# A hybrid decoder layer on one core: the first loads and the first product in another order, and the turned rows of x kept for the residual instead of being turned again

## The chip, the core and the metric

The kernel runs on one core of a Trainium2 chip, as one launch. The metric is device time in microseconds (us). The engines go by the profile's names: PE is TensorE (matrix products and transposes), DVE is VectorE, ACT is ScalarE, POOL is GpSimd, SP is SyncE, which here only issues DMAs. PE's weight loads (PEld) overlap its matmuls.

## What is computed

One inference step of one decoder layer: a prompt of 512 tokens and a sample group of 8 sequences with 4 tokens each, 544 token columns in all, with a model width of 1024.

```
h = RMSNorm_pre(x)
[x_r | q | k | v | g] = h @ W_in
A: x_r -> causal conv (4) -> RG-LRU (8 gate blocks, a scan over the tokens)
B: sliding-window attention, 8 query heads, 2 kv heads, sinks, T5 bias
m = (sigmoid(g_A) * (A @ W_A) + sigmoid(g_B) * (B @ W_B)) @ W_out
x = x + RMSNorm_post(m)                      # x itself is needed a second time here
u = RMSNorm_pre2(x) @ W_up ; causal conv (3)
x = x + RMSNorm_post2((gelu(u_gate) * u_val) @ W_down)
RMSNorm(x, g) = x * rsqrt(mean(x * x) + 1e-6) * g
```

The outputs are the layer's result for prompt and sample and the new recurrent, convolution and key/value states.

## The kernel before, in words

**Layout.** Activations are kept turned: a tile has 128 features on the partitions and the 544 tokens along the row, so the width is KD = 8 tiles. x arrives with tokens on the partitions, in five row blocks (TOK: four of 128 prompt tokens, one of 32 sample tokens), each in two halves of 512 features (x0_0, x0_1, ...). It has to be turned by PE against an identity, through PSUM.

**Products.** Every large product is done in split precision: weights and activations are each a high and a low part (wh, wl; hH, hL), and a weight column of 128 outputs takes three matmuls for each of the 8 k: wh by xh, wh by xl, wl by xh. The tokens are worked in two halves (HALF, 256 and 288 columns; from the lo stage on HALF2, 272 each), so a weight column is 24 matmuls for each half. The high part of a weight is a copy by ACT (`wsplit_hi`, L266), the low part a subtraction by DVE (`wsplit_lo`, L281), in two units of 4 k. `wload` (L246) loads a raw column block of 512 KB on SP's queue into one of five buffers (pool raw); `wclaim` (L256) has two columns loaded ahead.

**Stages.** Norm and turning; the input projection W_in (36 columns, order list L231 to L238, which starts with key, value and query columns 16, 18, 8, 9, 10); in between the attention units, the gates and scans of the RG-LRU, and the products ao (attention output) and lo (recurrent output); then out, the second norm, the up projection, the down projection and the end.

**The start.** `xload` (L357 to L361) issues the x halves on SP, with norm_mix_pre (rows_a) and the first weights among them. 18 dummy matmuls (WARM, tile ps_warm) run on PE meanwhile. `xsquares` (L404) makes sums of squares (ACT tile jk, DVE tile jv), `xrstd` (L412) the factor 1/rms (ss), `xscale` (L417) multiplies each row by it: in tokens-on-partitions form the factor is one number per partition. Then for each k two transposes write ps_ta (L448), and `hsplit` (L431 to L434) makes hH (ACT) and hL (DVE) with the norm's weight pv. The first product, column 16, has an order of its own in `mmhalf` (L315). `norm_b` (L451) does the other 288 tokens later: squares at one tick, factor and scaling at the next, then ps_tb (L461) and hsplit.

**Order.** PE's order is written out by hand throughout (manual_schedule), ACT's and DVE's in the mixer too. `step` (L331) issues one half product and calls `tick` (L194), which splits the next weights and lets side generators go on that were entered with `start_at(t, gen)` (L183); work put on the lists late and last comes after that. SP and POOL take their work in the order in which the program issues it; a waiting instruction holds all behind it on its engine.

**Tables.** `attn_tables` (L544) builds the prompt's bias tables: ps_ohp on PE, rvec on DVE, then on POOL's queue rscr, rrep (both in DRAM) and one btab for each pair of heads (L581). `sample_tables` (L556) makes the sample's bias: 16 copies lt from rel4 on POOL, the tile ohs by DMA, and ps_bs on PE.

**x a second time.** `x_again` (L995 to L1008) reads the row blocks of x again during the lo stage (tile xx, in the raw buffers, L998), turns them on PE (pxx, L1004: 40 transposes in ten groups of four) and copies them to x1[0..7] (L1008, half by ACT, half by DVE). x1 is the residual after the out stage.

PSUM has 3 banks for products (PM) and 5 for the rest (PX); the slots S (52 of 568 columns) hold most activations.

Of the kernel before, what the change touches and what calls it, by code (L numbers as in the profile page):

```python
# [17 lines left out]
P = 128  # L18
# [56 lines left out]
WARM = 18  # L75
# [48 lines left out]
def hawk_step(ctx, tc, I, O):  # L124
# [190 lines left out]
    def mmhalf(ps, key, X, a, ks=range(KD)):  # L315
        n = X.half[a][1] - X.half[a][0]
        if key == order[0] and a == 0:

            for j, (i0, i1) in enumerate(((0, 0), (1, 0), (0, 1))):
                for k in ks:  # L320
                    mm(ps[:, :n], wunits[2 * wpos[key] + k // 4][i0][:, k % 4, :], X.get(k, a, i1),
                       j == 0 and k == 0, j == 2 and k == KD - 1)
            return
        for k in ks:
            wh, wl = (wunits[2 * wpos[key] + k // 4][j][:, k % 4, :] for j in range(2))
            xh, xl = X.get(k, a, 0), X.get(k, a, 1)
            mm(ps[:, :n], wh, xh, k == 0, False)
            mm(ps[:, :n], wh, xl, False, False)
            mm(ps[:, :n], wl, xh, False, k == KD - 1)

    def step(key, X, a, done, target=None, look=2, quick=False):  # L331


        ps = PM("pm" + "_".join(str(z) for z in key) + f"_{a}")
        if quick:
# [27 lines left out]
    xload(0)  # L363
    xload(1)
    nc.sync.dma_start(out=rows_a[0:8, :], in_=I["norm_mix_pre"].rearrange("o (k p) -> (o k) p", p=P))
# [5 lines left out]
    for i in (2, 3, 4):  # L371
        wload(i)
    relx = cp.tile([NBK + 1, NH], F32, name="relx")
    pool.memset(relx, 1.0)
    pool.dma_start(out=relx[0:NBK, :], in_=I["rel_bias"])
    ohp = T("ohp")[:NBK + 1, 0:3 * WIN]
    pool.dma_start(out=ohp, in_=I["c_ohp"])
    for r, nme in ((8, "norm_mix_post"), (16, "norm_ffn_pre"), (24, "norm_ffn_post")):
        pool.dma_start(out=rows_a[r:r + 8, :], in_=I[nme].rearrange("o (k p) -> (o k) p", p=P))
# [6 lines left out]
    pe.transpose(ps0[:, 0:8], rows_a[0:8, :], ident[0:8, 0:8])  # L386
    G_PRE, G_POST, G_FPRE, G_FPOST, C_W, C_B, C_BR, C_BI, C_LAM = 0, 8, 16, 24, 32, 64, 72, 80, 88
# [49 lines left out]
    xsquares(1)  # L437
    xrstd(0, 2)
    split = [wsplit_hi(u) for u in wclaim(2)]
    xscale(0, "av")  # L440
    xscale(1, "vv")
    dve.tensor_copy(pv[:, 0:8], ps0[:, 0:8])
    for u in split:
        wsplit_lo(*u)
    for k in range(KD):
        ps = (PM if k in (5, 6) else PX)(f"ps_ta{k}")
        for i in range(2):
            pe.transpose(ps[:, i * P:(i + 1) * P], xtile(i, k), ident)  # L448
        hsplit(k, 0, ps[:, :256])

    def norm_b():  # L451
        last.extend(lambda i=i: xsquares(i) for i in (2, 3, 4))
        yield
        last.append(lambda: xrstd(2, 5))
        last.extend(lambda i=i, e=e: xscale(i, e) for i, e in ((2, "av"), (3, "av"), (4, "vv")))
        yield
        for k in range(KD):
# [4 lines left out]
            late.append(lambda k=k, ps=ps: hsplit(k, 1, ps[:, :288]))  # L462
# [74 lines left out]
    for t in range(DT):  # L537
        pool.dma_start(out=rel4[32 * t:32 * t + 32, :], in_=I["rel_bias"])
# [379 lines left out]
    start_at(1, norm_b())  # L918
    start_at(2, attn_tables())
# [75 lines left out]
    def x_again(i):  # L995
        t0, n, src = TOK[i]
        x_i = RAW(f"xx{i}")
        nc.sync.dma_start(out=x_i[:n, :], in_=src)  # L998
        yield 2 + i // 4
        for kk in range(2):  # L1000
            px = PX(f"pxx{i}_{kk}")
            for j in range(4):
                k = 4 * kk + j
                pe.transpose(px[:, j * P:j * P + n], x_i[:n, k * P:(k + 1) * P], ident[:n, :n])  # L1004
            yield
            for j in range(4):
                k = 4 * kk + j
                (dve.tensor_copy if j % 2 else act.copy)(x1[k][:, t0:t0 + n], px[:, j * P:j * P + n])  # L1008

    for i in range(5):  # L1010
        start_at(now[0] + 3 + 2 * i, x_again(i))
# [837 lines left out]
```

## Time and profile before

| | |
|---|---|
| median of 3 runs | 1002.92 us (1002.29 to 1003.08) |
| profiled execution | 1003.73 us |
| its span | 1002.0 us |
| busy: PE, DVE, ACT, POOL | 988.9, 732.0, 579.4, 151.0 us |
| first transposes of x (ps_ta) | 11.07 us after the span's start |
| lo stage | 335.66 to 390.40 us |
| mean DMA rate | 133 GB/s |

The span is the profiled execution from its first to its last instruction; the execution's own time holds another 1.7 us around it. In a row of the chain of waits the first number is the start, the second the length, then the engine, tile and line. In a row of the timeline an operation and its shape follow (out <- in, partitions x elements), and in brackets the idle time of the engine before it with what ended it. In a row that groups instructions the three durations are the least, the median and the greatest in ns. In a row of the windows each engine has its busy time with the number of instructions, then the granted PE clock, the mean busy share of the 16 DMA engines and GB/s.

### The profile page before, as it was taken

The numbers are of one execution on the slowest core, as the hardware profiler recorded it, in microseconds if no ns is written. First come the engines' busy times: TensorE is split into PE (matmuls) and PEld (weight loads), VectorE is DVE, ScalarE is ACT, GpSimd is POOL, SyncE is SP. The second block draws the span as 40 slices with busy tenths as digits, with TensorE's granted clock in tenths as the row PEclk, the third lists the DMA queues.
The fourth block names the chain that finished last, engine by engine and source line by source line (L and its number), as shares of the span: only waits on it lengthen the run. The fifth ranks groups of instructions, "written<-read, shape, count | busy, mean of one in ns | idle before, by whom it ended". The sixth has DMA issues, their size and how long they took to land.

```text
span 1002.0 us, 20195 instructions
## 1 busy us (share of the span) xinstructions
PE 988.9 (99%) x7837; PEld 978.5 (98%) x7837; DVE 732.0 (73%) x1555; ACT 579.4 (58%) x1422; POOL 151.0 (15%) x270
## 2 busy tenths in 40 slices
PE   8999999999999999999999999999999999999997
PEld 7999999999999999999999999999999999999996
DVE  6476687545846555589777788888888888887865
ACT  6444455469358535456776756565656565656652
POOL 3131010002304432110001111111111111110004
PEclk9999999999999999999999999999999999999999
DMA  7743223333322345327245858586867676767712
GB/s 211 231 150 93 64 77 105 99 91 94 102 68 85 106 138 148 105 66 210 71 116 124 193 124 192 125 191 127 189 133 184 139 177 145 171 160 167 216 45 90
DMA packets 207687, 133.40 MB, mean 133 GB/s; under 512 B 6546, under 2 KB 194306, under 8 KB 207560
## 3 DMA queue, kind: packets, MB, share of 16 engines
q1 hardware_dynamic: 197944, 112.20, 39.4%
q0 software_dynamic: 9600, 17.90, 11.3%
q10 hardware_dynamic: 48, 2.03, 0.5%
q8 instruction: 61, 1.00, 0.4%
q14 instruction: 34, 0.28, 0.1%
HBM read 111.82 MB, written 9.14 MB: 121 GB/s over the span
## 4 chain that ended last, share of the span: by engine, by line
PE 92%; DVE 3%; ACT 2%; DMA 2%; issue 0%; SPq 0%; ACTq 0%; DVEq 0%
PE pmin L165 22%; PE pmdn L165 16%; PE pux L1400 15%; PE puy L1400 7%; PE pq L1400 6%; PE pmout L165 5%; PE pmao L165 5%; PE pmlo L165 4%; PE puz L1400 4%; PE pg L165 1%; PE psc L165 1%; PE pvp L165 1%; DMA raw_up_s<-in_w_up_dram 1%; DMA raw_in<-in_w_in_dram 1%; PE pt L701 1%; PE ptok L165 1%
## 5 line engine op out<-in xcount | busy, mean ns | idle before, releaser
L165 PE MATMUL pmin<-hH,wh_in 128*128 128x256 f32 (+1 forms) x576 | 167.8, 294 | 0.0
L165 PE MATMUL pmin<-hH,wl_in 128*128 128x256 f32 (+1 forms) x576 | 164.7, 288 | 0.0
L165 PE MATMUL pmin<-hL,wh_in 128*128 128x256 f32 (+1 forms) x576 | 164.6, 288 | 0.0
L165 PE MATMUL pmdn<-fH,wh_dn 128*128 128x256 f32 (+1 forms) x448 | 129.2, 288 | 0.2 <-DVE ft L174 0.2
L165 PE MATMUL pmdn<-fH,wl_dn 128*128 128x256 f32 (+1 forms) x448 | 129.2, 288 | 0.2 <-DVE wl_dn L168 0.2
L165 PE MATMUL pmdn<-fL,wh_dn 128*128 128x256 f32 (+1 forms) x448 | 129.1, 288 | 0.0
L177 DVE SCALAR_TENSOR_TENSOR uc<-u,fv,uc 128x560 f32<-128x560 f32 x128 | 102.0, 797 | 13.3 <-ACT uc L1431 13.2
L165 PEld LDWEIGHTS pmin<-hH,wh_in 128*128 128x128 f32 x576 | 108.9, 190 | 1.9 <-issue 1.2
L165 PEld LDWEIGHTS pmin<-hL,wh_in 128*128 128x128 f32 x576 | 108.1, 188 | 0.0
L165 PEld LDWEIGHTS pmin<-hH,wl_in 128*128 128x128 f32 x576 | 107.9, 188 | 0.0
L165 PEld LDWEIGHTS pmdn<-fH,wh_dn 128*128 128x128 f32 x448 | 84.5, 189 | 0.6 <-issue 0.6
L165 PEld LDWEIGHTS pmdn<-fH,wl_dn 128*128 128x128 f32 x448 | 84.4, 188 | 0.4 <-DVE wl_dn L168 0.4
L165 PEld LDWEIGHTS pmdn<-fL,wh_dn 128*128 128x128 f32 x448 | 84.3, 188 | 0.0
L1526 ACT COPY u<-pux 128x272 f32<-128x272 f32 x52 | 20.1, 387 | 86.1 <-PE pux L1400 86.1
L168 DVE TENSOR_TENSOR u<-puy,u 128x240 f32<-128x240 f32 (+2 forms) x78 | 24.6, 344 | 49.8 <-PE puy L1400 32.1
L174 DVE TENSOR_TENSOR ft<-ft,pmdn 128x256 f32<-128x256 f32 (+1 forms) x104 | 45.2, 436 | 16.7 <-PE pmdn L165 16.1
L277 ACT ACTIVATE wh_in<-raw_in 128x512 fp32r<-128x512 f32 x72 | 44.2, 629 | 19.3 <-PE pmin L165 8.4
L282 DVE TENSOR_TENSOR wl_in<-raw_in,wh_in 128x512 fp32r<-128x512 f32 x72 | 48.2, 683 | 0.8 <-ACT wh_in L277 0.8
L1431 ACT ACTIVATE uc<-u,fv 128x560 f32<-128x560 f32 x64 | 48.2, 754 | 0.0
L664 ACT ACTIVATE s<-s,st 128x256 f32<-128x256 f32 (+1 forms) x32 | 15.2, 475 | 50.4 <-DVE st L661 43.0
L168 DVE TENSOR_TENSOR wl_dn<-raw_dn,wh_dn 128x512 fp32r<-128x512 f32 x56 | 38.3, 684 | 0.0
L1326 POOL DMA_DIRECT2D raw_up_s<-raw_up_s x26 | 22.7, 874 | 102.9 <-issue 5.2
(776 smaller groups left out, 3404.3 us busy)
## 6 DMA issues: line engine op xcount, KB each, us to landing
raw_in<-in_w_in_dram SPq DMA_DIRECT2D x36, 512.0 KB
raw_dn<-in_w_down_dram SPq DMA_DIRECT2D x56, 256.0 KB
raw_up_s<-in_w_up_dram SPq DMA_DIRECT2D x26, 512.0 KB
raw_up_s<-raw_up_s POOLq DMA_DIRECT2D x26, 256.0 KB, 5.9
raw_ao<-in_w_attn_o_dram SPq DMA_DIRECT2D x8, 512.0 KB
raw_lo<-in_w_lru_o_dram SPq DMA_DIRECT2D x8, 512.0 KB
raw_out<-in_w_out_dram SPq DMA_DIRECT2D x8, 512.0 KB
x1d<-x SPq DMA_DIRECT2D x8, 272.0 KB
```

Of the source, the lines that this page charges most:

```text
L165: pe.matmul(out, l, r, start=start, stop=stop)
L168: dve.tensor_tensor(out=out, in0=a, in1=b, op=ALU.subtract)
L174: dve.tensor_tensor(out=out, in0=a, in1=b, op=ALU.add)
L177: dve.scalar_tensor_tensor(out=out, in0=a, scalar=s_, in1=b, op0=op0, op1=op1)
L277: act.activation(hl[0], raw, AF.Copy)
L282: (eng or dve).tensor_tensor(out=hl[1], in0=raw, in1=f32(hl[0]), op=ALU.subtract)
L664: act.activation(s3[:, j, :], s3[:, j, :], AF.Exp, bias=ng[:, j:j + 1], accum_out=sm[:, j:j + 1])
L701: pe.transpose(pt[:, (2 * ch + j) * P:(2 * ch + j + 1) * P], s3[:, j, ch * P:(ch + 1) * P], ident)
L1326: pool.dma_start(out=w["p4"], in_=w["p2"], accum_op=ALU.add)
L1400: pe.matmul(ps[:, :HN], w, x, start=start and k == 0 and i == 0, stop=stop and k == 3 and i == 2, skip_group_check=True)
L1431: act.activation(yt[j][:, 0:FLATU], u[:, 0:FLATU], AF.Copy, scale=fv[:, j:j + 1])
L1526: act.copy(e[nm_], z)
```

## The change

1. *First loads.* SP loads norm_mix_pre ahead of the halves of x1 and no longer behind them. The small loads relx, ohp and three norm weights go from POOL's queue to SP's, ahead of weights 3 and 4; the four loads rel4 go from POOL's to SP's queue.
2. *Dummy matmuls.* WARM goes from 18 to 12; 11 more (KEEP) follow the transpose of norm_mix_pre.
3. *First product.* x0_0, x1_0, x0_1 are scaled by DVE and x1_1 by ACT, ahead of the weight's split; the low parts of column 16 are made by POOL, pv is copied by ACT. The first product's matmuls stand among the transposes ps_ta: the transposes of k, then wh by hH of k-2, then wh by hL of k-3, and all of wl by hH at the end.
4. *ps_ta.* Two k share one PSUM tile (four tiles in all), which stay until they are copied. In the built program the transposes of an odd k wait for the hL of the even k in the same tile, and the hH of an odd k for that hL too.
5. *Kept rows.* The turned, scaled rows are copied from PSUM to xn[0..7]: 8 copies of 128x256 (keep_a) and 8 of 128x288 (keep_b), half by ACT, half by DVE.
6. *Unscaled.* `unscale` takes 1/ss on DVE, sends it to DRAM turned (rmsd, 5 x 128 numbers) and back broadcast over the partitions (rms_full, 128x544), both on SP; POOL multiplies each xn by it and sends it to DRAM (xdram), 272 KB each. On POOL this stands between the first and the second btab.
7. *x a second time.* `x_again` becomes 8 loads from xdram into x1; the loads xx, the 40 transposes and the 40 copies go.

```diff
-WARM = 18
+WARM = 12
+KEEP = 11
...
     xload(0)
+    nc.sync.dma_start(out=rows_a[0:8, :], in_=I["norm_mix_pre"]...)
     xload(1)
-    nc.sync.dma_start(out=rows_a[0:8, :], in_=I["norm_mix_pre"]...)
     wload(0)
     wload(1)
...
     pe.transpose(ps0[:, 0:8], rows_a[0:8, :], ident[0:8, 0:8])
+    for z in range(KEEP):
+        mm(pw[:, (z % 4) * P:(z % 4 + 1) * P], ones, ident, True, True)
...
     xsquares(1)
+    act.copy(pv[:, 0:8], ps0[:, 0:8])
     xrstd(0, 2)
-    split = [wsplit_hi(u) for u in wclaim(2)]
-    xscale(0, "av")
-    xscale(1, "vv")
-    dve.tensor_copy(pv[:, 0:8], ps0[:, 0:8])
-    for u in split:
-        wsplit_lo(*u)
+    u0, u1 = wclaim(2)
...
+    scale0(0, 0)
+    scale0(1, 0)
+    act.activation(xt[1, 1][:, 0:512], xt[1, 1][:, 0:512], AF.Copy, scale=ss[:, 1, 1:2])
+    scale0(0, 1)
+    first_ps = PM("pm_first")
...
+    ps_ta = []
+    wsplit_lo(*wsplit_hi(u0), eng=pool)
+    for k in range(KD + 3):
+        if k < KD:
+            if k % 2 == 0:
+                ps_ta.append(PX(f"ps_ta{k // 2}"))
+            ps = ps_ta[-1][:, k % 2 * 256:k % 2 * 256 + 256]
+            for i in range(2):
+                pe.transpose(ps[:, i * P:(i + 1) * P], xtile(i, k), ident)
+            hsplit(k, 0, ps)
+        if k == 1:
+            wsplit_lo(*wsplit_hi(u1), eng=pool)
+        if 0 <= k - 2 < KD:
+            first_mm(k - 2, 0, 0, start=k == 2)
+        if 0 <= k - 3 < KD:
+            first_mm(k - 3, 0, 1)
     for k in range(KD):
-        ps = (PM if k in (5, 6) else PX)(f"ps_ta{k}")
-        for i in range(2):
-            pe.transpose(ps[:, i * P:(i + 1) * P], xtile(i, k), ident)
-        hsplit(k, 0, ps[:, :256])
+        first_mm(k, 1, 0, stop=k == KD - 1)
...
+    def keep_a(k):
+        (dve.tensor_copy if k % 2 else act.copy)(xn[k][:, 0:256], ps_ta[k // 2][:, k % 2 * 256:k % 2 * 256 + 256])
+
+    def keep_b(k, ps):
+        (act.copy if k % 2 else dve.tensor_copy)(xn[k][:, 256:NT], ps[:, :288])
+
+    def unscale():
+        dve.reciprocal(rms, ss[:, 1, :])
+        nc.sync.dma_start(out=rmsd.rearrange("i p -> p i"), in_=rms)
+        full = S("rms_full")
+        a = rmsd[:, :]
+        nc.sync.dma_start(out=full[:, 0:NT], in_=bass.AP(a.tensor, a.offset, [[0, P], [1, NT]]))
+        yield 2
+        for k in range(KD):
+            pool.tensor_tensor(out=xn[k][:, 0:NT], in0=xn[k][:, 0:NT], in1=full[:, 0:NT], op=ALU.mult)
+            pool.dma_start(out=xdram[k], in_=xn[k][:, 0:NT])
...
     def norm_b():
         last.extend(lambda i=i: xsquares(i) for i in (2, 3, 4))
+        last.extend(lambda k=k: keep_a(k) for k in range(4))
         yield
+        last.extend(lambda k=k: keep_a(k) for k in range(4, KD))
         last.append(lambda: xrstd(2, 5))
...
-            late.append(lambda k=k, ps=ps: hsplit(k, 1, ps[:, :288]))
+            late.append(lambda k=k, ps=ps: (hsplit(k, 1, ps[:, :288]), keep_b(k, ps)))
...
     start_at(1, norm_b())
+    start_at(6, unscale())
...
-    def x_again(i):
-        t0, n, src = TOK[i]
-        x_i = RAW(f"xx{i}")
-        nc.sync.dma_start(out=x_i[:n, :], in_=src)
-        yield 2 + i // 4
...
-    for i in range(5):
-        start_at(now[0] + 3 + 2 * i, x_again(i))
+    def x_again():
+        for k in range(KD):
+            nc.sync.dma_start(out=x1[k][:, 0:NT], in_=xdram[k])
+        yield
+
+    start_at(now[0] + 3, x_again())
```

## What was predicted, with its working

> **What bounds the kernel now.** I read the page's head and its chain first, then the chain cut to the stretches that the change touches, then those stretches engine by engine.
>
> ```profile
> span 1002.0 us, 20195 instructions
> PE 988.9 (99%) x7837; PEld 978.5 (98%) x7837; DVE 732.0 (73%) x1555; ACT 579.4 (58%) x1422; POOL 151.0 (15%) x270
> PE 92%; DVE 3%; ACT 2%; DMA 2%; issue 0%; SPq 0%; ACTq 0%; DVEq 0%
> ```
>
> TensorE is busy in 99% of the span. So a matmul taken off it is worth its own time, and anything that lets it starve costs in full. The change does both: it takes transposes out of the lo stage (a gain that can be read off), and rebuilds the first 35 us, where TensorE starves already.
>
> The chain through the lo stage, 335.66 to 390.40:
>
> ```profile
> 335.66 15.00 PE pmlo L165 x120
> 350.67 0.44 PE pxx L1004 x4
> ...
> 361.00 0.44 PE plr L904 x4
> ...
> 368.50 4.50 DMA xx<-in_x_prompt_dram
> 373.00 0.14 issue
> 373.14 0.63 PE pxx L1004 x4
> ...
> 386.82 0.36 PE pxx L1004 x4
> 387.19 3.21 PE pmlo L165 x24
> 390.40 9.62 PE pmout L165 x77
> ```
> ```profile
> 339.78 0.37 SPq L254 DMA_DIRECT2D raw_lo<-in_w_lru_o_dram  x1
> ```
>
> Ten groups of pxx (the second turning of x) stand in it between blocks of products, and once TensorE waits for a row tile (xx) that comes late. The last row is SP's issue of a late lo weight.
>
> The start, chain first:
>
> ```profile
> 9.26 1.15 ACT wh_in L277 x2
> 11.07 2.90 PE ps_ta L448 x16
> 24.09 2.02 PE ps_tb L461 x12
> 31.18 12.62 PE pmin L165 x96
> 67.39 0.85 PE ps_bs L165 x4
> ```
>
> Up to the first product the path is load, norm, scale, turn; from there it is TensorE in a row, with ps_bs (sample bias, from the tile ohs) in its order.
>
> **The lo stage: gain 5.8.** 390.40 - 335.66 = 54.74 us. The 16 half products are 384 matmuls; at 15.00/120 = 0.125 they need 48.0. Two plr groups stay, 0.88. The rest, 54.74 - 48.0 - 0.88 = 5.86, is ten groups of transposes (eight of 0.44, two of 0.36: 4.24), the wait for xx (about 0.9), and slower refills. In the new program no turning is left; 8 loads of x1 (272 KB each, from DRAM) stand on SP in front of one of the last lo weights. That one went out at 339.78 and its product runs after 373, some 30 us later. They move as many bytes as the x loads that go.
>
> ```profile
> 335.66:390.40 54.74, 53.82 (x435) 53.15 (x434) 29.67 (x70) 24.15 (x61) 18.42 (x19) 1.00 0.43 129
> 372.00:373.00 1.00, 0.22 (x2) 0.00 (x0) 0.00 (x0) 0.00 (x0) 0.51 (x1) 1.00 1.23 371
> ```
>
> The DMA share is 0.43 there, and 371 GB/s was moved in the best us: 2.2 MB take 6 us at that rate, 17 at the stage's mean of 129. Either fits. The 40 copies that go from ScalarE and VectorE were on engines half idle: nothing. I take -5.8; the least is -4.9 (transposes 4.24 and 0.66 of the wait), the most -5.9.
>
> **The start: cost 5.0.** Its rows:
>
> ```profile
> 9.39 1.28 DVE L425 TENSOR_SCALAR x<-x,ss 128x512 f32<-128x512 f32 x3
> 11.55 3.03 ACT L433 ACTIVATE hH<-ps_ta,pv 128x256 fp32r<-128x256 f32 x8 [0.53 <-PE ps_ta L448]
> 12.05 3.23 DVE L177 SCALAR_TENSOR_TENSOR hL<-ps_ta,pv,hH 128x256 fp32r<-128x256 f32 x8
> 14.80 0.47 DVE L177 SCALAR_TENSOR_TENSOR hL<-ps_ta,pv,hH 128x256 fp32r<-128x256 f32 x1
> 18.73 0.42 DVE L168 TENSOR_TENSOR kL<-pmin,kH 128x256 fp32r<-128x256 f32 x1 [0.43 <-ACT kH L599]
> 21.66 1.34 ACT L423 ACTIVATE x<-x,ss 128x512 f32<-128x512 f32 x2 [0.83 <-DVE ss L177]
> 21.66 1.67 DVE L425 TENSOR_SCALAR x<-x,ss 128x512 f32<-128x512 f32 x4
> 27.80 1.28 DVE L282 TENSOR_TENSOR wl_in<-raw_in,wh_in 128x512 fp32r<-128x512 f32 x2
> L501 DVE COPY fv<-ps_rows x1: 415/415/415, 51.9 to 51.9; 128x256 f32<-128x256 f32 x1
> ```
>
> (a) *Earlier turning.* Both x tiles of the first transpose are now first on VectorE and wh follows on ScalarE, so the first turn can start at about 9.39 + 2 x 0.43 = 10.25 instead of 11.07; rows_a ahead of x1 puts up to 0.4 of that back. The 11 added dummy matmuls lie in TensorE's idle stretch before it: nothing, if rows_a lands by about 6.5 (dummies are 0.17 each, 22 instructions, 3.7 us); else up to 0.8.
>
> (b) *Two tiles in one bank.* Before, eight ps_ta had eight PSUM tiles, and hL went every (3.23 - 0.475)/7 = 0.39 us. Now two k share a tile, and the built program ties them: the odd transposes wait for the even hL, the odd hH too. A pair becomes a chain: hL 0.48, turn to hH 0.48 (11.55 - 11.07), hH to hL 0.50 (12.05 - 11.55), next hL 0.39: 1.85 where 0.78 was. With hL0 at 10.25 + 0.98 = 11.23, and the second half of wh_in_16 in between on ScalarE (+0.5), hL7 starts at 11.23 + 4 x 1.85 - 0.39 + 0.5 = 18.7, not 14.80: +3.9. At best, with steps of 0.3 to 0.4 each, a pair is 1.5: +2.5. The first product, spread among the turns, ends 9 matmuls after hL7.
>
> (c) *Copies kept.* keep_a puts four copies 128x256 on each of VectorE and ScalarE ahead of the second norm's scaling. A like copy is 0.41, so 1.3 to 1.7; I take 1.7. From hL7 to the scaling was 21.66 - 14.80 = 6.86; so the scaling comes at 18.7 + 6.86 + 1.7 = 27.3, and its ScalarE part ends 1.34 later, 28.6. ps_tb stood at 24.09: **+4.5**. TensorE gets there at about 27 (19.2, 9 matmuls, another product of 3, ps_ohp, a third of 3), so it is idle for 1.6 us: VectorE and ScalarE bound this stretch, and copies count in full.
>
> (d) *keep_b.* In the split of the second half xn1 and xn3 on ScalarE wait for hL on VectorE, and hH2 queues behind them. From hH0 I follow the two engines step by step (0.35 to 0.5 each): wl_10's first half is done at about 35.8 (27.80 + 0.64 before, with 2.7 us of slack to the product at 31.18). TensorE wants it at 28.6 + 2.02 + 3.06 + 2.02 = 35.7. Slack gone, no wait or 0.5: **+4.5 to +5.0**. The rel4 loads on SP and the lt copies come ahead of the bias tables' chain on GpSimd, which waits for rvec behind the same scaling, and moves like TensorE: nothing beyond.
>
> I take +5.0; from below +3.0 (best pairs, 1.3 for copies), from above +6.5.
>
> Rule against row on KEEP:
>
> ```profile
> 11.00:12.00 1.00, 0.93 (x8) 0.93 (x9) 0.95 (x2) 0.47 (x3) 0.68 (x2) 0.96 1.03 379
> 12.00:13.00 1.00, 1.00 (x7) 1.00 (x6) 0.95 (x3) 1.00 (x5) 0.94 (x8) 0.50 1.08 332
> 15.00:16.00 1.00, 1.00 (x9) 1.00 (x8) 1.00 (x3) 1.00 (x4) 0.00 (x0) 0.83 1.22 290
> ```
>
> The granted clock falls to 0.50 from about 12 to 15.3, after an idle TensorE up to 11.07. The Trainium skill ("TensorE: Matmul & The Clock Gate", Part 1: The HAM clock gate) says that the clock halves after an idle window of about 3.4 us and returns after a busy one; the trace agrees, and by that rule KEEP could hold full clock. Since (b) is bound by hH and hL, full clock would save at most the transposes' half, 4 x 0.18 = 0.7 by the rows; I leave it in the range.
>
> **The unscaling on GpSimd: cost 0.5.** After btab0 GpSimd gets 8 multiplications 128x544 and 8 DMAs; vn, btab1, kout, vout and ohs queue behind.
>
> ```profile
> 42.12 0.76 POOL L581 DMA_DIRECT2D btab<-rrep  x1 [12.73 <-DMA rrep<-rscr]
> 55.31 0.54 POOL L561 DMA_DIRECT2D ohs<-in_c_ohs_dram  x1
> DMA to landing us min/median/max: 2.5/2.5/2.5
> L881 POOL TENSOR_TENSOR xc<-xc,lt x8: 1400/1442/1947, 251.5 to 328.9; 128x568 f32<-128x568 f32 x8
> DMA rscr<-rvec: 3.7, 1
> ```
>
> Start S: btab0 ends at 42.9 + 5 = 48; the factor goes out as rmsd (640 elements of 4 bytes) and comes back as rms_full, issued about 41 and 45 after rows like rscr (3.7 each): 49. So S = 49. Then 8 x (1.45 + 0.75) = 17.6, then vn, btab1, kout, vout and ohs (2.9 together), landing 2.5: ohs is there at 49 + 17.6 + 2.9 + 2.0 = 71.5 to 73.5. TensorE wants it at 67.39 + 5.0 = 72.4: slack of 12 us goes to about none. I take 0.5; the bounds are 0 and 5 (the GpSimd rival).
>
> SP is held between rmsd and rms_full for about 4 us; the weight behind it, (in, 14), comes after four more weight columns of some 6 us each: nothing.
>
> The Trainium skill ("DMA: Bandwidth & Descriptors", Specifications) gives 512 B as the least transfer for line rate, with a read-modify-write below: it speaks against rmsd's 4-byte pieces. No row here shows such a store.
>
> **Sum.** -5.8 + 5.0 + 0.5 = -0.3 on the profiled execution's 1003.73 (span 1002.0 and 1.7 around it): 1003.4. The runs' median, 1002.92, is 0.8 lower; so 1002.6, rounded up for the waits left at nothing: **1002.8**.
>
> **Rivals.**
> - *Front nearly free* (0.22): the tie within a bank is cheaper (pairs of 1.2, hL7 at 16.2) and the copies fit into VectorE's and ScalarE's waits, of which the rows show 0.43 and 0.83. Then the front costs 1 to 2.5: 1002.9 - 5.8 + 2 = 999.1. For: TensorE had 0.8 of slack at ps_tb. Against: the waits in the program.
> - *GpSimd late* (0.18), the slower side: rmsd lands late or the multiplications run at 1.95 like the slowest xc (+4), ohs after 72.4 + x, and TensorE stands x at ps_bs. It decides from S = 50; x of 4 to 5 gives 1002.8 + 4.3 = 1007.1. For: the slack is gone by my sum, and rrep on the same queue took 13 us (12.73 in btab's row). Against: TensorE may itself be later.
> - *Half clock* (0.09): the first product is spread thin over 9 us, and if the clock stays at 0.50 to about 26, the following product costs up to 2.8 more, of which 1.6 is idle anyway; and 1 more if the next goes too: 1005.
> - *The gain isn't had* (0.07): x1's loads hold back the last lo and the first out weights, and the wait for xx comes back as one for a weight: up to 4.5 as xx took: 1006.
>
> Forecast: 0.44. **Range.** From the front nearly free to GpSimd late: 999.0 to 1007.5. It leaves out the cheaper end of the first and the dearer end of the second. **Chances**, with 0.2% (2 us) as what a measurement of this kernel tells from no change: faster 0.26 (0.22 and 0.04 of the forecast's own low end), same 0.40, slower 0.34 (the other three).
>
> **What would show it.** Right: no pxx, and lo 48 to 49 us long; hL in steps of 0.4 and 1.45 by turns, hL7 at 18.7; scaling at 27.3; TensorE idle 1 to 2 us ahead of ps_tb; product (in, 10) done near 39; ohs's issue near 70 with ps_bs soon after. Wrong: hL evenly spaced, ps_tb before 26, a wait of DMA ohs at ps_bs over 1 us, or idle TensorE in lo or out.

## The result and the profile after

| | before | after |
|---|---|---|
| median of 6 runs (lowest to highest) | 1002.79 us (1002.29 to 1003.4) | 1021.78 us (1016.58 to 1023.58) |
| ratio to before | | 1.0176 (95% interval 1.016 to 1.0191) |
| profiled execution, its span | 1003.73, 1002.0 us | 1022.56, 1020.7 us |

The change makes the kernel slower by 19 us, and the prediction (1002.8, at most 1007.5) was wrong. The runs after also spread over 7 us where those before spread over 1. A run more than 1.5% above the fastest of its kernel is slow and is left out of the ratios here and below; there is one, of 1028.75 us, in small_tiny.

The head of the page of after, and the shares of its chain:

```profile
span 1020.7 us, 20162 instructions
PE 995.2 (98%) x7807; PEld 982.4 (96%) x7807; DVE 736.2 (72%) x1541; ACT 578.8 (57%) x1411; POOL 164.7 (16%) x279
PE 87%; DVE 5%; DMA 2%; ACT 2%; issue 2%; SPq 0%; POOL 0%; ACTq 0%; DVEq 0%; POOLq 0%
```

PE had 30 matmuls less and was "busy" 6.3 us longer, at a lower granted clock (0.987 over the span, 0.997 before); its share of the chain fell from 92% to 87%. Rows of the chain of after, cut to the first 90 us and to the lo stage:

```profile
9.60 0.34 PE ps_ta L461
...
13.48 0.69 PE ps_ta L461 x2
14.17 0.43 PE pm_first L166 x2
...
36.17 16.95 issue
53.14 8.10 DMA btab<-rrep
...
70.45 3.53 DVE s L717 x2
...
75.40 5.71 PE pmin L166 x24
...
88.62 0.85 PE ps_bs L166 x4
```
```profile
357.28 23.99 PE pmlo L166 x192
...
406.20 3.88 PE pmout L166 x31
```

Before, PE itself carried the chain from 31 us on. Now it leads through rrep (GpSimd issues it at 35.05 and has it 17 us later), the first btab (8.10 us) and then VectorE, up to 75 us. The same places of both programs, first starts as the trace groups them by tile (us):

| | before | after | later by | added since the row above |
|---|---|---|---|---|
| first transposes (ps_ta) | 11.1 | 9.2 | -1.9 | -1.9 |
| transposes of the second half (ps_tb) | 23.9 | 29.1 | 5.2 | 7.1 |
| first attention scores (psc) | 43.6 | 50.0 | 6.4 | 1.2 |
| sample bias (ps_bs) | 67.2 | 88.5 | 21.3 | 14.9 |
| lo stage (pmlo) | 335.5 | 357.1 | 21.6 | 0.3 |
| out stage (pmout) | 390.2 | 406.0 | 15.8 | -5.8 |
| up projection (pux) | 523.2 | 539.1 | 15.9 | 0.1 |
| the last matmul of the up projection (pux) | 948.1 | 966.9 | 18.8 | 2.9 |
| span | 1002.0 | 1020.7 | 18.7 | -0.1 |

Four terms: the start costs 6.4, the stretch from psc to ps_bs 14.9, the lo stage gives 5.8 back, and 2.9 go at the end of the up projection. These are single profiles: in the runs below with the same first loads and dummies the first turn lies between 9.2 and 10.9, so the row psc of one profile can be off by more than 1 us. What PE waited for in the first 110 us of after (total us, times, longest):

```profile
PE ps_ta L461 <- DVE hL L178: 4.1, 4, 1.6
PE pt L746 <- DVE s L717: 3.7, 2, 2.9
PE pmin L166 <- DVE qL L169: 2.6, 2, 1.7
PE psc L166 <- DVE s L178: 2.5, 1, 2.5
```

The first row is the tie between two k in one PSUM tile. The other three, 8.8 us, are the stretch from 58 to 76: in order of time, 2.5 and 1.7 us follow the late first btab, and 0.9, 2.9 and 0.9 come from 70 to 75, behind VectorE. The rest of its 14.9, some 6 us, goes with half clock, as the windows show: about as many matmuls (191 for 190 before), and no other wait (columns as in the prediction: length, busy time of PE, PEld, DVE, ACT, POOL, then granted clock, DMA share, GB/s):

```profile
58.00:62.00 4.00, 1.46 (x11) 1.22 (x10) 0.62 (x2) 0.00 (x0) 0.00 (x0) 1.00 0.48 80
62.00:66.00 4.00, 2.26 (x13) 2.06 (x14) 2.59 (x7) 2.21 (x10) 2.61 (x2) 0.67 1.01 272
66.00:70.00 4.00, 4.00 (x19) 3.73 (x18) 4.00 (x5) 0.00 (x0) 3.98 (x5) 0.50 0.62 162
70.00:74.00 4.00, 0.33 (x2) 0.14 (x1) 3.93 (x5) 0.00 (x0) 3.98 (x6) 0.93 0.67 254
```

From 66 to 70 PE is busy throughout and gets 19 matmuls done where it got 33 from 50 to 54, at a granted clock of 1.00: that is the half clock. From 64 on VectorE and GpSimd are both busy nearly without a gap.

**What delays the factor and the bias tables.** The queue of SP in after, then windows while rmsd is on its way, and the packets of 53 to 58.2 by queue (number, MB, share of the 16 engines' time; q0 has btab's packets, q1 rmsd's pieces):

```profile
42.97 0.37 SPq L485 DMA_DIRECT2D rmsd<-rms  x1
58.19 0.34 SPq L488 DMA_DIRECT2D rms_full<-rmsd  x1
```
```profile
46.00:49.00 3.00, 3.00 (x25) 3.00 (x24) 1.44 (x3) 1.30 (x3) 0.00 (x0) 1.00 0.46 9
49.00:53.00 4.00, 4.00 (x33) 4.00 (x33) 0.00 (x0) 1.97 (x3) 0.00 (x0) 1.00 0.41 32
```
```profile
q0 software_dynamic: 43, 0.17, 86.0%
q1 hardware_dynamic: 175, 0.00, 2.0%
```

Between the store of rmsd (2.5 KB, 640 pieces of 4 bytes) and the load that waits for it lie 15.2 us. For much of that time the engines are marked busy at 41% and more, and move 9 to 32 GB/s. From 53 to 58.2 they are not busy with the pieces, whose share is 2%: 43 packets of btab hold 86%, that is 5.2 x 16 x 0.86 / 43 = 1.7 us each. Before, from 44.6 to 48.8, 160 packets of that queue (0.52 MB) held 33.8%, 0.14 us each. (Ahead of 53 the pieces share their queue with packets of a weight, whose share can't be told from theirs.) rrep and this btab, on another queue, come late as well: GpSimd waited 12.73 us for rrep before and 16.96 now, and btab takes 8.1 us where the prediction reckoned with 5 for S, the start of the multiplications.

**What the multiplications do to VectorE.** GpSimd, then VectorE, in after:

```profile
67.55 2.64 POOL L491 TENSOR_TENSOR xn<-xn,rms_full 128x544 f32<-128x544 f32 x2
...
71.27 2.62 POOL L491 TENSOR_TENSOR xn<-xn,rms_full 128x544 f32<-128x544 f32 x2
```
```profile
64.40 2.62 DVE L283 TENSOR_TENSOR wl_in<-raw_in,wh_in 128x512 fp32r<-128x512 f32 x2
...
67.76 2.46 DVE L175 TENSOR_TENSOR st<-st 128x2 f32<-128x2 f32 x1
...
70.45 3.53 DVE L717 TENSOR_SCALAR s<-s,st 128x128 f32<-128x128 f32 x2
```

The same three kinds in before, grouped by shape (the last two numbers of each row are busy us and mean ns):

```profile
L282 DVE TENSOR_TENSOR wl_in<-raw_in,wh_in 128x512 fp32r<-128x512 f32 x3 | 2.0, 682 | 0.0
L672 DVE TENSOR_SCALAR s<-s,st 128x128 f32<-128x128 f32 x2 | 0.5, 283 | 0.0
L174 DVE TENSOR_TENSOR st<-st 128x2 f32<-128x2 f32 x3 | 0.5, 155 | 0.0
```

An instruction on 128x2 takes 0.155 us before and 2.46 in after; it ends at 70.22, and GpSimd's pair of multiplications ends at 67.55 + 2.64 = 70.19. Likewise the next: 70.45 + 3.53 = 73.98, and 71.27 + 2.62 = 73.89. VectorE's instruction does not run slowly, it stands until GpSimd's is through.

### The profile page after: what moved, and what is told of

Its sections match the earlier page's. It is cut to its first block, busy times and chain, and to the rows that moved or that the text cites. A ratio compares the mean times of both kernels' runs of the same rounds, so it can differ in the third digit from the quotient of the medians.

```text
span 1020.7 us, 20162 instructions
## 1 busy us (share of the span) xinstructions
PE 995.2 (98%) x7807; PEld 982.4 (96%) x7807; DVE 736.2 (72%) x1541; ACT 578.8 (57%) x1411; POOL 164.7 (16%) x279
## 3 DMA queue, kind: packets, MB, share of 16 engines
q0 software_dynamic: 9952, 20.06, 12.1%
## 4 chain that ended last, share of the span: by engine, by line
PE 87%; DVE 5%; DMA 2%; ACT 2%; issue 2%; SPq 0%; POOL 0%; ACTq 0%; DVEq 0%; POOLq 0%
PE pmin L166 18%; PE pmdn L166 16%; PE pux L1435 15%; PE puy L1435 7%; PE pq L1435 6%; PE pmout L166 5%; PE pmao L166 5%; PE pmlo L166 5%; PE puz L1435 4%; PE pg L166 1%; PE pvp L166 1%; PE psc L166 1%; DMA raw_up_s<-in_w_up_dram 1%; DMA btab<-rrep 1%; PE pt L746 1%
## 5 line engine op out<-in xcount | busy, mean ns | idle before, releaser
L1561 ACT COPY u<-pux 128x272 f32<-128x272 f32 x52 | 20.1, 386 | 82.5 <-PE pux L1435 82.5
L175 DVE TENSOR_TENSOR ft<-ft,pmdn 128x256 f32<-128x256 f32 (+1 forms) x104 | 45.3, 436 | 15.9 <-PE pmdn L166 15.1
L709 ACT ACTIVATE s<-s,st 128x256 f32<-128x256 f32 (+1 forms) x32 | 15.2, 475 | 65.2 <-DVE st L706 57.9
```

The costliest lines, as they stand in the source:

```text
L175: dve.tensor_tensor(out=out, in0=a, in1=b, op=ALU.add)
L709: act.activation(s3[:, j, :], s3[:, j, :], AF.Exp, bias=ng[:, j:j + 1], accum_out=sm[:, j:j + 1])
L1561: act.copy(e[nm_], z)
```

## The experiments

Theory: two parts of the unscaling, each by itself, hold up the stretch from psc to ps_bs: the store in 4-byte pieces, which is slow to complete and makes transfers beside it late, and GpSimd's multiplications, which block VectorE. The tie in one PSUM tile sets the cost of the start. Rivals: the cost is GpSimd's queue alone (whatever stands behind the multiplications there), or the start alone, or the copies. Ratios are to the kernel before on the same chip; run 1 further down means experiment 1, and so on.

**1. The store in rows of 512 bytes** (rows_store). The factor is turned on PE first.

```diff
-        nc.sync.dma_start(out=rmsd.rearrange("i p -> p i"), in_=rms)
+        yield
+        ps = PX("ps_rms")
+        pe.transpose(ps[:5, 0:P], rms, ident)
+        yield
+        rmst = cp.tile([5, P], F32, name="rmst")
+        act.copy(rmst, ps[:5, 0:P])
+        nc.sync.dma_start(out=rmsd, in_=rmst)
```

> The changed kernel (1021.8 us) with rmsd stored in 5 rows of 512 bytes instead of 640 pieces of 4: TensorE turns the 128x5 factors, ScalarE copies them, and only then SP stores them (some 6 us later than in the changed kernel). Theory A (the 4-byte store loads the DMA engines from 43 to 58 us, so that rrep takes 17.8 us for 13.6 and btab0 8.1 for 5.4): rrep is back at about 13.6 and btab0 at 5.5, TensorE has no wait at the first scores, and the time falls by 10 to 15, to 1007 to 1012. What stays is the front (+6.2 at the first scores) and GpSimd's multiplications. Rival B (the bias tables are late because rvec is late behind the slower front, and no slack was there): rrep moves little, the time stays above 1017.

Measured: 1020.37 us, ratio 1.0172 (1.0157 to 1.0187). SP's wait for the store and, further on, the chain:

```profile
SPq L494 <- DMA rmsd<-rmst: 1.7, 1, 1.7
```
```profile
75.39 13.35 DMA mk<-in_c_msk_dram
```

The store leaves at 49.93 and the load behind it at 52.93: the same 2.5 KB are through in 3.0 us instead of 15.2, rrep lands after 10.9 us, and ps_bs comes at 77.4 instead of 88.5. But the time is hardly better. VectorE is held as in after (s, at 60.44: 3.59 us for two instructions of 283 ns), and mk, the last of the small loads behind the multiplications and the eight stores on GpSimd's queue, lands 13.35 us after its issue at 75.39; PE waits 6.1 us for it. The lo stage starts at 354.5, 2.6 earlier than in after. One of two causes was taken away, and the multiplications alone cost nearly as much. But most of it comes by another way than in after: from psc (52.7) to ps_bs are 24.7 us, only 1.2 more than without any unscaling (run 2), and from ps_bs to the lo stage 277.1, for 268.3 before. That is mk, which GpSimd issues 19 us later than before because the multiplications and stores stand ahead of it. It then meets a copy that ACT's queue makes, of the caches from DRAM to DRAM, two of 992 KB:

```profile
75.11 1.29 ACTq L638 DMA_DIRECT2D out_dram<-in_cache_win_k_dram  x1
```

Before, ohs and mk were out (55.31 to 56.4) and landed 2.5 us later, ahead of that copy (62.54). That the copy makes mk slow is argued from the times, since no run moves it; but in before a btab issued at 66.48, during the copy, took 9.3 us as well, and in tiny_mult 10.0.

**2. No unscaling at all** (no_unscale): no rmsd, no rms_full, no multiplication.

```diff
-        dve.reciprocal(rms, ss[:, 1, :])
-        nc.sync.dma_start(out=rmsd.rearrange("i p -> p i"), in_=rms)
-        full = S("rms_full")
-        a = rmsd[:, :]
-        nc.sync.dma_start(out=full[:, 0:NT], in_=...)
...
-            pool.tensor_tensor(out=xn[k][:, 0:NT], in0=xn[k][:, 0:NT], in1=full[:, 0:NT], op=ALU.mult)
```

> The changed kernel without the unscaling: no reciprocal, no rmsd, no rms_full, no multiplications on GpSimd; xn goes to DRAM as it is, so that the residual is the scaled x (that part of the computation is left out). Theory A with C (the store and the multiplications together make all of the loss between 50 and 88 us: +15.0 there): front +6.2, lo -5.8, end +0 to 2.8: 1003 to 1006. The distance to the kernel with rows of 512 bytes is what the multiplications cost by VectorE slowed beside them and by ohs late: 3 to 8. Rival B (tables late in themselves): a wait for btab0 stays, 1008 or more.

Measured: 1009.69 us, 1.0065 (1.0048 to 1.0081). So the unscaling costs 12.4 us: after is 1021.78 - 1002.79 = 18.99 above its before, this kernel 1009.69 - 1003.12 = 6.57. From psc (51.2) to ps_bs (74.7) are 23.5 us, as before (23.6). The time is above the 1003 to 1006 expected, but PE has no wait for the first btab, which the rival named; psc is 7.6 us later than before, 1.2 more than in after.

**3. Multiplications of one column** (tiny_mult), on top of rows_store: the eight instructions, loads and stores stay.

```diff
-            pool.tensor_tensor(out=xn[k][:, 0:NT], in0=xn[k][:, 0:NT], in1=full[:, 0:NT], op=ALU.mult)
+            pool.tensor_tensor(out=xn[k][:, 0:1], in0=xn[k][:, 0:1], in1=full[:, 0:1], op=ALU.mult)
```

> The kernel with rmsd in rows of 512 bytes (1020.4), but each multiplication on GpSimd is of one column only (so the residual keeps the scaled x in the other columns; that part of the computation is left out). Same waits, same DMAs, 10 us less of GpSimd's time and no VectorE held beside it. If the multiplications are what makes mk late and VectorE slow (TensorE waited 6.1 for kL behind mk): 9 to 11 us faster, 1009 to 1011. Rival (the 2.2 MB of xdram on GpSimd's DMA queue make mk late): mk lands late still, above 1016.

Measured: 1009.36 us, 1.0058 (1.0038 to 1.0078); ps_bs at 73.7, no wait of PE in the stretch over 0.2. Against rows_store that is 17.25 - 6.14 = 11.1 us for the multiplications' size alone. The edit takes away both of their effects, the hold on VectorE and GpSimd's time: ohs goes out at 63.5 for 74.3 in rows_store, and mk lands in 3.8 us.

**4. One column, but the store in 4-byte pieces** (small_tiny): the edit of 3 on after itself, without that of 1.

```diff
         nc.sync.dma_start(out=rmsd.rearrange("i p -> p i"), in_=rms)
...
-            pool.tensor_tensor(out=xn[k][:, 0:NT], ...)
+            pool.tensor_tensor(out=xn[k][:, 0:1], ...)
```

> The changed kernel, 4-byte store and all, with each multiplication on GpSimd of one column only (the rest of the residual keeps the scaled x; that part of the computation is left out). Beside the same kernel with the store in rows (1009.4) it shows the price of the 4-byte store alone. Theory A1 (the store makes rrep and btab0 7 us late, and TensorE then stands and falls to half clock): 3 to 6 us above it, 1012 to 1015. Theory A2 (the multiplications are all of the loss, the store only fills slack): 1009 to 1010.5.

Measured: 1019.4 us (1013.38 to 1022.61), 1.0152 (1.0116 to 1.0188). No long multiplication is left, and the loss is nearly that of after: 15.77 - 6.14 = 9.6 above tiny_mult, to some 4 us either way. It comes out at another place, since ohs is among what is late:

```profile
73.04 12.08 DMA ohs<-in_c_ohs_dram
```
```profile
71.79 1.30 ACTq L632 DMA_DIRECT2D out_dram<-in_cache_win_k_dram  x1
```

PE waits 10.0 us at ps_bs. Here too the copy of the caches is beside it: the factor is back at 59.4 for 54.6 in tiny_mult, GpSimd issues ohs at 73.04 for 63.50, and it lands after 12.1 us for 3.9. So either cause alone costs some 10 us, and both together (after) not 20 but about 12: the waits lie on top of one another, which is why taking one away (1) looked like nothing. In after itself ohs and mk took 3.7 to 4.0 us, since the copy came behind them (83.77); there the waits are those shown with the result. The runs of this kernel spread over 9 us and those of tiny_mult over 4, but late_small, with the 4-byte store as well, over 1.4: that the store makes the spread is not shown.

**5. The unscaling 20 ticks later** (late_small), away from the bias tables.

```diff
-    start_at(6, unscale())
+    start_at(26, unscale())
```

> The changed kernel with one edit: the whole unscaling (4-byte store, broadcast load, multiplications, stores to DRAM) starts at tick 26 instead of 6, so that on GpSimd it stands behind both first btab, ohs, mk and btab2, in a stretch where no table is on its way. Theory A with C (the store of 4-byte pieces and the multiplications do harm only because they meet the bias tables and the first attention units): rrep is back at 11 to 14 us, no wait at the first scores, ps_bs at 67.4 + 6 to 7; front +6.2, lo -5.8, and the 2.9 at the end of the up projection if that belongs to the new way of x: 1003 to 1007. Rival B (the slower front alone makes tables and TensorE miss each other): over 1010.

Measured: 1022.17 us, 1.0191 (1.0172 to 1.0209). ps_bs is free (75.0, rrep after 11.0), and the loss comes back later:

```profile
126.00:130.00 4.00, 4.00 (x35) 4.00 (x34) 1.87 (x5) 1.05 (x3) 0.00 (x0) 1.00 0.00 0
```
```profile
SPq L488 <- DMA rmsd<-rms: 9.0, 1, 9.0
```
```profile
PE pmin L166 <- ACT xr L866: 9.9, 1, 9.9
```

The store leaves at 120.94 and the load behind it at 130.41, 9.5 us later, though no other transfer is under way: the DMA share is 0.20 from 122 to 123 and nothing after that. The pieces themselves are cheap: from 120.9 to 122.4 they hold the 16 engines at 20.1%, 0.3 us of each. So the store is slow to complete by itself; what it does from 123 to 130 no record shows. What PE waits for now is xr, whose first columns GpSimd sets after the multiplications and stores (134.5 to 149.5). Here the rival has its part: GpSimd's queue.

**6. The tie in one bank, alone** (front_only and front_far). front_only is parts 1 to 4 of the change (no xn, no unscale, x turned again as before); front_far is the same with k and k+4 in one PSUM tile instead of k and k+1.

```diff
-    start_at(6, unscale())
...
-    start_at(now[0] + 3, x_again())
+    for i in range(5):
+        start_at(now[0] + 3 + 2 * i, x_again(i))
```
```diff
-            if k % 2 == 0:
-                ps_ta.append(PX(f"ps_ta{k // 2}"))
-            ps = ps_ta[-1][:, k % 2 * 256:k % 2 * 256 + 256]
+            if k < 4:
+                ps_ta.append(PX(f"ps_ta{k}"))
+            ps = ps_ta[k % 4][:, k // 4 * 256:k // 4 * 256 + 256]
```

> Only parts 1 to 4 of the change: first loads, dummy matmuls, first product and four shared PSUM tiles; x is turned a second time as before, and nothing is kept or unscaled. Theory: the front without the kept copies costs +4 at the first scores (tie 3.9, copies 1.7 and the 0.5 of keep_b gone), tables move along: 1006 to 1007. Rival (the kept copies, not the tie, make the front late): within 1.5 of 1002.8.

> Parts 1 to 4 alone (1009.2 measured) with k and k+4 in one PSUM tile. Theory (the tie of neighbours costs 3.6 up to hL7, as the scaling showed): 3 to 4 us faster, 1005 to 1006; what is left over 1002.8 is the first product spread thin at half clock and rel4 behind the other loads on SP. Rival (after the tie goes, TensorE at half clock is the bound): less than 2 faster.

Measured: front_only 1009.15 us, 1.0063 (1.0048 to 1.0078), psc at 49.5; front_far 1004.28 us, 1.0011 (1.0001 to 1.002), psc at 43.6, as before. The tie costs 6.03 - 1.06 = 5.0 us. The first loads, the dummies and the new order of the first product bring nothing measurable: with the tie gone they cost 1.1.

**7. The same edit in the whole change** (bank_far); keep_a reads the rows from there.

```diff
...
-            ps = ps_ta[-1][:, k % 2 * 256:k % 2 * 256 + 256]
+            ps = ps_ta[k % 4][:, k // 4 * 256:k // 4 * 256 + 256]
```

> The changed kernel with k and k+4, not k and k+1, in one PSUM tile: same four tiles, but the transposes no longer wait for the hL just before. Theory of the prediction (the tie costs 4 us up to hL7): hL comes every 0.4 us, hL7 at about 15, the scaling of the second half at about 23.5 instead of 28.3, the first scores at about 46 instead of 50. As the 4-byte store stays, the time falls by only the same 4, to about 1018. Rival (the front's delay is absorbed by the wait for btab0, or the dense start itself is what is slow): above 1020.

Measured: 1025.2 us, 1.0219 (1.0197 to 1.0242): slower than after, though psc comes 3.6 earlier (46.4, with the first turn at 10.6 for 9.2). The 4-byte store now leaves at 39.42 and meets rrep earlier; SP waits 18.5 us for it:

```profile
SPq L488 <- DMA rmsd<-rms: 18.5, 1, 18.5
```
```profile
PE psc L166 <- DVE s L178: 7.0, 1, 7.0
```

GpSimd waits 20.8 us for rrep, and PE for the first bias table. What the start gained was lost at the next step.

**8. The start as before, the rest of the change** (old_front): copies kept, rows of 512 bytes, multiplications on GpSimd at tick 26, x1 loaded.

```diff
-        ps = (PM if k in (5, 6) else PX)(f"ps_ta{k}")
+        if k < 4:
+            ps_ta.append(PX(f"ps_ta{k}"))
+        ps = ps_ta[k % 4][:, k // 4 * 256:k // 4 * 256 + 256]
...
+    start_at(26, unscale())
```

> The other half of the change alone: the start as before (loads, order of the first product, dummy matmuls), x kept from the norm (k and k+4 in one PSUM tile), rmsd in rows of 512 bytes, the unscaling at tick 26, x1 loaded from DRAM. Theory (kept copies 0 to 1.7 at the start, lo -5.8, tables untouched): 997 to 999, or 1000 to 1002 if the wait of 2.9 at the end of the up projection belongs to the new way of x. Rival (the copies and stores cost what they save): 1003 or more.

Measured: 1017.32 us, 1.0138 (1.0122 to 1.0154). ps_bs at 69.0; the loss lies where the multiplications are (125.7 to 140.2). PE's wait there (pt turns the scores s), and VectorE's groups from 125 to 160:

```profile
PE pt L734 <- DVE s L705: 8.0, 2, 5.3
```
```profile
L282 DVE TENSOR_TENSOR wl_in<-raw_in,wh_in 128x512 fp32r<-128x512 f32 x7 | 7.9, 1127 | 0.0
L174 DVE TENSOR_TENSOR st<-st 128x2 f32<-128x2 f32 x2 | 3.4, 1697 | 0.6 <-ACT st L698 0.6
```

SP waits 0.9 us for the store here, and GpSimd's queue holds nothing that PE waits for. What PE waits for is VectorE, with means of 1127 and 1697 ns for instructions of 682 and 155. That is VectorE held by GpSimd, without the rival's help.

**9. The multiplications on VectorE, in the lo stage** (dve_old with the start as before, dve_far with the new start, k and k+4 in one PSUM tile and rel4 back on GpSimd's queue; both with the store of run 1). The rows go out scaled, x1 is loaded and then multiplied.

```diff
-            pool.tensor_tensor(out=xn[k][:, 0:NT], in0=xn[k][:, 0:NT], in1=full[:, 0:NT], op=ALU.mult)
...
+        for k in range(KD):
+            mul(x1[k][:, 0:NT], x1[k][:, 0:NT], full[:, 0:NT])
+            yield
```

> The start as before; x kept from the norm and stored scaled, 1/ss stored in rows of 512 bytes; in the lo stage x1 is loaded and multiplied by VectorE (8 times 128x544), so that GpSimd multiplies nothing. If GpSimd's multiplications holding VectorE are what makes every version lose 10 us or more, this one has no such loss: lo -5.8, kept copies +1.8, wait at the end of the up projection +2.9: 1001 to 1003; without that wait 998 to 1000. Rival (multiplications hurt wherever they stand, or the copies at the start cost more): above 1005.

> The changed kernel mended in four places: k and k+4 in one PSUM tile, 1/ss stored in rows of 512 bytes, rel4 on GpSimd's queue again, the multiplications on VectorE in the lo stage. Front +1.1 (measured without copies) and copies +2 to +3, lo -5.8, +2.9 at the end of the up projection: 1003 to 1005. If it is beyond 1007, something of the new front beside the tie still costs.

Measured: dve_old 1003.86 us, 1.0004 (0.9995 to 1.0013); dve_far 1002.62 us, 0.9992 (0.9984 to 1.0001). In dve_far the eight multiplications cost VectorE 8.6 us of a stage in which it has them to spare:

```profile
L172 DVE TENSOR_TENSOR x<-x,rms_full 128x544 f32<-128x544 f32 x8 | 8.6, 1076 | 0.0
```

The lo stage of dve_far takes 48.9 us (337.0 to 385.9). So the 19 us are gone, and the gain of 5.8 is still not there as time: out starts 4.3 us before that of before, and the span is 1.2 shorter. 3.0 of it goes at the end of the up projection.

**10. Copies and stores, nothing read** (keep_only): the kernel before, with the rows kept and stored and x turned again.

```diff
+        last.extend(lambda k=k: keep_a(k) for k in range(4))
...
+        for k in range(KD):
+            pool.dma_start(out=xdram[k], in_=xn[k][:, 0:NT])
```

> The start as before, x kept and stored scaled to DRAM, 1/ss stored in rows, but nothing of it read: x is turned a second time as before. It prices the kept copies and the stores alone: copies +1.8 (first scores at 45.4 for 43.6), so 1004 to 1005.5. It also asks where the wait of 2.9 at the end of the up projection comes from: there, if keeping x in the slots and storing it makes it; not there, if the new loads of x1 or the missing transposes do.

Measured: 1006.76 us, 1.0032 (1.002 to 1.0044). Keeping costs 3.1 us: psc is 1.6 later (45.2), ps_bs 2.7 (69.9). The wait at the end of the up projection is 0.3.

**11. Is that wait set by the number of DMAs on SP?** (dve_far_pad, before_pad) dve_far and the kernel before get some small loads on SP's queue, which go out between 27 and 33 us.

```diff
+    for z in range(6):
+        nc.sync.dma_start(out=cp.tile([NH, 1], F32, name=f"pad{z}"), in_=I["attn_sink"].rearrange("o h -> h o"))
```

> dve_far with six more small loads (32 bytes each) on SP's queue, early in the mixer; everything else is as there. If the wait of about 2.9 us at the end of the up projection (TensorE's pux for VectorE's wl) comes from the count of DMAs on SP ahead of it, it goes or moves: 1002.6 - 2.9 = 999.7 us. Rival: it belongs to the loads of x1 from DRAM themselves or to the transposes that are missing, so the wait stays at 2.5 to 3.0 and the time at 1002.6, plus at most 0.5 for the six loads.

> The kernel before with five more small loads (32 bytes each) on SP's queue, early in the mixer. If the count of DMAs on SP sets the wait at the end of the up projection, it appears here too: 1002.8 + 2.9 = 1005.7 us, with TensorE's pux waiting 2.5 to 3.0 for VectorE's wl. Rival: the loads of x1 or the missing transposes are the cause; then there is no such wait and the time stays at 1002.8, plus at most 0.5.

Measured: dve_far_pad 1002.26 us, 0.9989 (0.998 to 0.9998), with the wait at 2.7; before_pad 1003.05 us, 0.9995 (0.9986 to 1.0004), without it. Five or six DMAs more do not set it. dve_far_pad has the lowest time of the study, 0.1% below the kernel before and not clearly below dve_far.

The wait, in after, on PE and on VectorE:

```profile
945.54 0.39 PE L1435 MATMUL pux<-t1H,wl_s_p 128*128 128x272 f32 x1 [2.94 <-DVE wl_s_p L169]
```
```profile
907.61 0.69 DVE L175 TENSOR_TENSOR p<-raw_up_s,raw_up__12109 128x512 f32<-128x512 f32 x1 [1.28 <-DMA raw_up_s<-in_w_up_dram]
```

Up to 900 us the loads of after follow those of before at a constant 15.6 to 15.8 us. Then one raw_up_s lands some 1.3 us late, with a DMA share of 1.12 from 904 to 906 (1.16 at the like place of before), and the next loads, which wait for buffers that VectorE frees, go out 1.2 to 2 us later than that distance. Every kernel that loads x1 in the lo stage has this wait (2.5 to 3.0), no other has more than 0.3. Why a load at 900 us depends on that stays open.

## Why the prediction was wrong, point by point

**The lo stage: right.** -5.8 predicted, 54.74 - 48.92 = 5.82 measured, and no wait for a weight. That rival is out.

**The start: mechanism right, size short.** +5.0 predicted, 6.4 measured at psc.

(a) The first turn came at 9.2, earlier than the 10.25 of the text; in the other runs with these loads it came at 9.2 to 10.9.

(b) is the term that was mis-sized. A pair of k was put at 1.85 (1.46 and 0.39); it took 2.62:

```profile
12.94 0.48 DVE L178 SCALAR_TENSOR_TENSOR hL<-ps_ta,pv,hH 128x256 fp32r<-128x256 f32 x1 [0.40 <-ACT hH L432]
14.71 0.48 DVE L178 SCALAR_TENSOR_TENSOR hL<-ps_ta,pv,hH 128x256 fp32r<-128x256 f32 x1 [1.29 <-ACT hH L432]
15.56 0.48 DVE L178 SCALAR_TENSOR_TENSOR hL<-ps_ta,pv,hH 128x256 fp32r<-128x256 f32 x1 [0.37 <-ACT hH L432]
...
19.96 0.48 DVE L178 SCALAR_TENSOR_TENSOR hL<-ps_ta,pv,hH 128x256 fp32r<-128x256 f32 x1 [1.29 <-ACT hH L432]
```

The steps alternate as forecast, but as 1.77 and 0.85: the odd turn takes 0.69 on PE at half clock instead of 0.44, and the even turn stands behind it and two matmuls of the first product (0.43), which the 0.39 of an untied row did not contain. So hL7 starts at 19.96, not 18.7. The two runs of experiment 6 show that the tie is the cause (5.0 us). Beside this, the Trainium skill ("PSUM — Partial Sum Buffer", PSUM bank collisions raise a hardware error) asks that accesses of two engines be ordered by bank, not by address, which speaks against two k at work in one bank; the trace shows what that order costs here.

(c) Copies "in full", 1.7: under the tie they cost 0.5 to 1.0 (psc at 49.5 without them, in front_only, and 50.0 with them, where the first turn was 0.5 earlier), probably since TensorE at half clock is late by itself. Without the tie they cost 1.6 to 2.8 at psc (45.2 and bank_far's 46.4 against 43.6). The number was near, the place was not.

The dummies (KEEP) did not keep the clock: over the first 20 us it was 0.80, against 0.91 before.

**The unscaling: this step failed.** "I take 0.5; the bounds are 0 and 5"; run 2 gives 12.4, and runs 1, 3, 4, 5 and 8 its causes: the multiplications were counted as GpSimd's time alone, and the store of the factor as one of few large pieces. Three parts of it:
- *The factor's way through DRAM.* "after rows like rscr (3.7 each)" gave S = 49. The row was a wrong neighbour: rscr writes 8 rows of 384 numbers, rmsd 640 single ones. It took 15.2 us to the next step, S was 63.4, and rrep and btab beside it were late as well. The prediction had the rule of the Trainium skill ("DMA: Bandwidth & Descriptors", Specifications) on pieces under 512 B in hand and left it out of the range, because no row showed it. Run 1 shows what the pieces cost here: five rows of 512 bytes are through in 3.0 us. Whether the read-modify-write of that page lies behind it no run shows.
- *The multiplications.* Their own length was right (1.34 against 1.45). They were counted as GpSimd's time alone, and a row that would have told otherwise was in the trace of before, beside the one that was quoted. GpSimd multiplies xc from 251.52 to 252.93 and from 253.50 to 254.91; VectorE in that time and after it:

```profile
251.65 1.83 DVE L282 TENSOR_TENSOR wl_ao<-raw_ao,wh_ao 128x512 fp32r<-128x512 f32 x1
...
253.57 2.53 DVE L887 TENSOR_TENSOR_SCAN hs<-rg,xc 128x568 f32<-128x568 f32 x1
...
256.37 0.68 DVE L282 TENSOR_TENSOR wl_ao<-raw_ao,wh_ao 128x512 fp32r<-128x512 f32 x1
...
257.68 1.33 DVE L887 TENSOR_TENSOR_SCAN hs<-rg,xc 128x568 f32<-128x568 f32 x1
```

  Beside GpSimd's multiplications the same instructions take 1.83 and 2.53 us that take 0.68 and 1.33 without. Eight of them, back to back but for the issues, hold VectorE for some 10 us (an estimate, 8 x 1.34), and around 65 us PE waits for what VectorE makes. The Trainium skill ("SBUF — State Buffer", SBUF: two separate sides) says that VectorE and GpSimd share a port pair which one instruction holds to its end, for VectorE instructions with two SBUF inputs or in a fast mode; the trace agrees, with 2.46 us for an instruction of 0.155.
- *GpSimd late, the rival.* It named the right place (ps_bs) and the right side, with 4.3 us by a wait for ohs. In after there was no such wait: ohs was issued at 80.61, and PE came at 88.62, held by the late btab, by VectorE and by the clock. Its point of decision, S over 50, was passed by 13 us, and what it gave for itself, the 12.73 us of rrep, pointed at transfers, not at VectorE. Where only one of the two causes is left, the rival's wait is there, longer than it said: 6.1 us for mk (run 1) and 10.0 for ohs (run 4), with the copy of the caches beside it, which no case had.

**Half clock**, a rival at 0.09 for the first product, came in part: in the start, and again from 62 on after the waits (0.67 and 0.50), where it cost an estimated 6 us (14.9 less the 8.8 of the waits). The waits were not in the forecast, so their clock was not.

**The end of the up projection**, 2.9, was in no case.

## What to carry to other kernels

An idle GpSimd is not free: before elementwise work goes there, look in the trace at what VectorE's instructions take beside GpSimd's present ones, and price each GpSimd multiplication as VectorE time too. Price a small DMA by its pieces, not its bytes, and turn a column into rows on PE before it is stored. Ask of small loads that become late which large transfer they will then meet. And when one of two overlapping causes is removed and the time stays, remove the other one alone before either is cleared.

## What the runs showed of the hardware that was not expected

- A store of 2.5 KB in 640 pieces of 4 bytes keeps the load that waits for it back by 9.5 us with the DMA engines idle (late_small), by 15.2 in after and 19.0 in bank_far, against 3.0 in rows of 512 bytes. In after, packets of another queue beside it took 1.7 us of an engine each, for 0.14 before.
- Loads on GpSimd's queue that are under way with the copy of the caches (two of 992 KB) took 9.3 (btab, before), 10.0 (btab, tiny_mult), 12.1 (ohs, small_tiny) and 13.4 us (mk, rows_store); ohs and mk clear of it took 2.3 to 4.0.
- VectorE's smallest instruction with both inputs in SBUF can take 2.46 us (of 0.155) while GpSimd multiplies two 128x544 tiles.
- The clock halves without a long idle stretch: PE idle for 2.5 us before 61.8 and 1.7 before 64.5, with the six matmuls of psc in between, was enough for 0.50 from 66 to 70.
